# A decoder layer's sliding-window attention: the softmax reciprocals laid out in the odd slots, in a bank of the scores' ring

## The chip, the cores and the metric

The kernel runs on one core of a Trainium2 chip. The metric is the time of one execution on the device in microseconds (us); lower is better. The core's engines are TensorE (PE, with its weight loads PEld), VectorE (DVE), ScalarE (ACT), GpSimd (POOL) and SyncE (SP, which issues transfers). Each engine runs its instructions in the order of its own queue and waits there for semaphores of the others. TensorE writes its results into PSUM, of which this kernel uses eight banks of 128 x 512 float32; VectorE and ScalarE read them from there.

## The reference

One layer with two branches on x (1024 x 1024, float32). What matters here is the attention branch:

```python
proj = rmsnorm(x, norm_pre) @ w_in          # -> pool_u, pool_gate, q, k, v, attn_gate
# 8 heads of 64, 2 key/value heads, blocks of 128 queries, window 128, ALiBi bias, a sink per head
scores = einsum('bnqhgd,bnkhd->bnhgqk', q, kb) * 64 ** -0.5       # own and previous block of keys
scores = where(valid, scores + bias, -1e30)
probs = softmax(concatenate([scores, sink], -1), -1)[..., :-1]
attn_out = einsum('bnhgqk,bnkhd->bnqhgd', probs, vb) * silu(attn_gate)
pool_out = pool_mixer(pool_u, pool_w, pool_scale) * silu(pool_gate)
x = x + rmsnorm(concatenate([pool_out, attn_out], -1) @ w_out, norm_post)
```

## The kernel before

Matrix products run on pairs of float16 tensors (a high and a low part), three products for one of float32. The order of all engines' queues is the order of the program text (a manual schedule); the framework adds the semaphores.

After an opening part (norms, transposes, v, k and the first q), a loop runs over the slots s = 5 to 33. Each slot computes one projection tile (proj, L283: 24 products of 128 x 512 into one of two "acc" banks), in the order q, pool_gate, u, attn_gate, and threads a piece of the attention between. With n = (s - 5) // 2, the even slot and the odd slot behind it form pair n. In block terms, a pair does the following.

- Even slot: pv_land(n-2) (VectorE, L465) multiplies the values' product of block n-2 by what lies in cat; mask(n-1) (GpSimd, two selects L427 and L431); score_mm(n) (TensorE, L360: 24 products into four banks); then proj, and in its middle (after 12 of 24 products) `middle()`; behind proj score_land(n) (VectorE, L371 to L382, reads the four banks) and exps(n) (ScalarE, L389).
- Odd slot: turn(n) (ScalarE, L399), proj with `middle()`, pv_mm(n-1) (TensorE, L455), turn_low(n) (VectorE L404 and L411, a transposing transfer L408, and GpSimd's copy r at L413, which spreads the reciprocals of block n).

`middle()` first runs scales(): a transpose that spreads a weight block's bound (L82), then on VectorE a reduction and five tiny operations (L87, L73, L76, L77, L213), and on ScalarE the scaled copy of the weights (high_w, L219). It runs only in slots whose turn it is. Then, before the change in even slots, `divide(n - 1)`: TensorE transposes r (four transposes, L442) into a bank rb, and ScalarE copies rb, times a factor, into cat (L443). pv_land later multiplies that. Last, pool_mm (L508) runs where the pooling branch has something ready.

PSUM is dealt out like this: two "acc" banks; a ring of four under the tag "b" (`bank()`: score tiles, the pooling branch's products, half of the output); one bank "pv" for the values' product pvo and, before the change, for rb; one for spread. A ring hands its banks out in turn, and a tile waits until the last reader of its predecessor in that bank is done.

Of the kernel before, what the change touches and what calls it, by code (L numbers as in the profile page):

```python
# [9 lines left out]
F32 = mybir.dt.float32  # L10
# [9 lines left out]
P = 128  # L20
# [3 lines left out]
NB = S // P  # L24
# [11 lines left out]
def trunk(ctx: ExitStack, tc, x, w_in, pool_w, pool_scale, attn_sinks, w_out, norm_pre, norm_post, out):  # L36
# [16 lines left out]
    ps_pv = ctx.enter_context(tc.tile_pool(name="ps_pv", bufs=1, space=PSUM))  # L53
# [11 lines left out]
    def block_of(n):  # L65
        return slice(n * P, (n + 1) * P)

    def bank(name, n=512):
        return ps_b.tile([P, 512], F32, tag="b", name=name)[:, :n]
# [10 lines left out]
    def spread(m):  # L80
        t = ps_sp.tile([P, 512], F32, tag="sp", name="spread")[:, :P]
        nc.tensor.transpose(t, m.broadcast_to([P, P]), ident)  # L82
        return t

    def widest(t):
        a = col("amall")
        nc.vector.tensor_reduce(a, t, axis=AX.X, op=ALU.max)  # L87
        return a
# [132 lines left out]
    def low_w(ch):  # L221
        w, s = whl[ch], halves.pop(ch)
        nc.vector.scalar_tensor_tensor(  # L223
            w[:, 1], raws.pop(ch), s, w[:, 0], op0=ALU.mult, op1=ALU.subtract
        )
# [126 lines left out]
    def score_mm(n):  # L352
        k0 = 0 if n else 1
        for pr in range(2):
            banks = [bank("sc").rearrange("p (c b s) -> p c b s", c=2, b=2) for _ in range(2)]
            for ci in range(2):
                for i, (a, b) in enumerate(PASSES):
                    for kv in range(2):
                        rows = slice(kv * HD, (kv + 1) * HD)
                        nc.tensor.matmul(  # L360
                            banks[kv][:, ci, k0:, :],
                            qT[rows, a, 2 * pr + ci, block_of(n)],
                            kT[rows, b, (n - 1 + k0) * P : (n + 1) * P],
                            start=i == 0, stop=i == 2,
                        )
            att_sc[n, pr] = banks
# [29 lines left out]
    def turn(n):  # L396
        st, sums = att_s.pop(n)
        ph = att.tile([P, 2, 8, P], F16, tag="ph", name="ph")
        nc.scalar.activation(ph[:, 0], st[:, :, :P], AF.Copy, scale=4096.0)  # L399
        att_f[n] = (st, sums, ph)  # L400
# [19 lines left out]
    def mask(n):  # L420
        full = att_f.pop(n)
        if n == 0:
            att_p[n] = [(0, full)]
            return
        own = att.tile([P, 2, 8, P], F16, tag="own", name="own")
        f, o = (t.rearrange("p a j t -> p (a j) t") for t in (full, own))
        nc.gpsimd.affine_select(  # L427
            o, f, pattern=[[0, 16], [1, P]], compare_op=ALU.is_ge, fill=0.0,
            base=0, channel_multiplier=-1,
        )  # L430
        nc.gpsimd.affine_select(  # L431
            f, f, pattern=[[0, 16], [-1, P]], compare_op=ALU.is_ge, fill=0.0,
            base=-1, channel_multiplier=1,
        )
        att_p[n] = [(n, own), (n - 1, full)]


    def divide(n):
        r = att_r.pop(n)
        rb = ps_pv.tile([P, 512], F32, tag="pv", name="rb")  # L440
        for c in range(4):
            nc.tensor.transpose(rb[:, block_of(c)], r[:, block_of(c)], ident)  # L442
        nc.scalar.activation(  # L443
            cat[:, 4:8, block_of(n)], rb.rearrange("p (c t) -> p c t", t=P), AF.Copy, scale=vo
        )
# [17 lines left out]
    def pv_land(n):  # L463
        dst, pv = cat[:, 4:8, block_of(n)], att_o.pop(n)
        nc.vector.tensor_tensor(dst, pv.rearrange("p (c t) -> p c t", t=P), dst, op=ALU.mult)  # L465
# [18 lines left out]
    def pool_windows(c, half):  # L484
        ug = pool_in.pop((c, half))
        w = WINDOWS[c]
        cur, d = ug, 1
        while d < w:
            nxt = strip("win")
            lo = 2 * d - 1  # L490
            nc.vector.tensor_tensor(
                nxt[:, lo:], cur[:, lo:], cur[:, lo - d : PAD + 512 - d], op=ALU.add
            )
            cur = nxt
            d *= 2
        res = strip("res")[:, PAD:]
        nc.vector.scalar_tensor_tensor(
            res, cur[:, PAD:], 1.0 / w, ug[:, PAD:], op0=ALU.mult, op1=ALU.subtract
        )
        if half == 0:  # L500
            first = slice(PAD, PAD + w - 1)
            nc.vector.tensor_tensor(cur[:, first], cur[:, first], invc[:, : w - 1], op=ALU.mult)
            nc.vector.tensor_tensor(res[:, : w - 1], cur[:, first], ug[:, first], op=ALU.subtract)
        pool_out[c, half] = res
# [140 lines left out]
    with tc.manual_schedule(engines={ENG.PE, ENG.Activation, ENG.DVE, ENG.Pool, ENG.SP}):  # L645
# [125 lines left out]
        def load_next():  # L771
            ch = next(loads, None)
            if ch:
                load_w(ch)
# [9 lines left out]
        for s in range(5, last):  # L784
            ch, half = slots[s]
            n, odd = (s - 5) // 2, (s - 5) % 2
            if not odd:
                if 2 <= n <= NB + 1:
                    pv_land(n - 2)
                if 1 <= n <= NB:  # L790
                    mask(n - 1)
                if n < NB:
                    score_mm(n)
            elif n < NB:
                turn(n)
            if 20 <= s < 24:
                gate = cat[:, s - 20, :]
                nc.scalar.activation(gate, gate, AF.Silu)
            gates = list(pool_out)

            def sums():
                for key in list(pool_in):
                    pool_windows(*key)


            def lows():
                for c2 in list(halves):
                    low_w(c2)
                    load_next()


            def scales():
                for key in list(bounds):
                    if key[0] in ("wo", "c"):
                        spreads[key] = spread(bounds.pop(key))
                        if key[0] == "c":
                            scale_cat(key[1])
                        else:
                            pow2_of(widest(spreads.pop(key)), wop, wos, 14)
                            state["wo"] = True  # L820
                    elif first_slot[key] == s + 3:
                        spread_w((key,))
                        scale_w((key,))
                        high_w(key)

            def middle():
                if s < LATE:
                    scales()
                if not odd and 1 <= n <= NB:
                    divide(n - 1)  # L830
                for key in gates:
                    pool_mm(*key)

            ready = list(halves)
            if s < LATE:
                sums()
                lows()
                acc = proj(ch, half, middle)
            else:
                acc = proj(ch, half, middle, scales)  # L840
                sums()
                for c2 in ready:
                    low_w(c2)
                    load_next()
                if s >= 26 and wo_lo < wo_hi:
                    low_wo(wo_lo)
                    wo_lo += 1
            if odd and 1 <= n <= NB:
                pv_mm(n - 1)
            if odd and n < NB:  # L850
                turn_low(n)

            for c2 in order:
                if first_slot[c2] == s + 5:
                    bound_w(c2)

            if 9 <= s < 9 + KT:
                wo_raw["b", s - 9] = load_wo(s - 9)
            if 11 <= s < 11 + KT:
                bound_wo(s - 11)  # L860
            if s == 11 + KT:
                m = bounds["wo", 0] = col("wom")
                nc.vector.tensor_reduce(m, wom, axis=AX.X, op=ALU.max)
            if s >= 30:
                bound_cat(s - 30)
            if not odd and n < NB:
                score_land(n)
            for key in gates:
                pool_gate(*key)
            land_slot(ch, half, acc)  # L870
            if s >= 23 and wo_hi < KT:
                split_wo(wo_hi)
                wo_hi += 1
            if not odd and n < NB:
                exps(n)
            if s == 5 + 2 * NB + 1:
                open_late()
            if 21 <= s < 21 + KT:
                wo_raw["o", s - 21] = load_wo(s - 21)
            if s >= last - 2:  # L880
                load_res(s - last + 2)
# [47 lines left out]
```

## Time and profile before

| | |
|---|---|
| time, median of the runs | 342.42 us (lowest 341.96) |
| profiled execution | 341.63 us, its span 339.9 us |
| TensorE busy | 322.6 us, 95% of the span |
| VectorE, ScalarE, GpSimd busy | 198.3, 169.6, 66.1 us |
| chain that ended last | TensorE 60%, issue 14%, VectorE 10%, GpSimd 8%, ScalarE 5% |

The loop of slots with attention in them lies between about 61 and 190 us; the rest of the projections run to 250 us, and the output product to 335 us. Matmuls are pipelined, so the sum of their single times is more than the stretch they take; the start of one to the start of the next is the measure. In a timeline row the number in brackets is the engine's idle time just ahead of it, with the instruction that ended it.

### The profile page before, as it was taken

What the parts mean: (1) busy time and instruction counts of PE and PEld (TensorE: products, weight loads), DVE (VectorE), ACT (ScalarE), POOL (GpSimd) and SP (SyncE); (2) the same over time, 40 slices, a digit from 0 to 9 for tenths busy, and PEclk for the clock granted to TensorE, in tenths of its full rate; (3) what the DMA queues carried; (4) which work ended last, traced back from release to release, by engine and by line L of the source; (5) the groups of instructions that cost most, each with busy time, mean ns of one, the idle gap of its engine ahead of it and who ended that gap; (6) DMA issues with size and microseconds to landing.
All of it is one profiled execution on the core that took longest, in us unless ns stands there. A gap on an engine that the chain in (4) does not pass through costs nothing.

```text
span 339.9 us, 5053 instructions
## 1 busy us (share of the span) xinstructions
PE 322.6 (95%) x1913; PEld 166.8 (49%) x1913; DVE 198.3 (58%) x423; ACT 169.6 (50%) x368; POOL 66.1 (19%) x73
## 2 busy tenths in 40 slices
PE   4789999999999999999979999999999999999993
PEld 2688556545445445454434444444444444444442
DVE  4977871537697444796979678833753633310122
ACT  5867831275657675888394573326543442211011
POOL 1101303000142343132405000000000233312330
PEclk9999999999999999999999999999999999999999
DMA  8976240002437376385631690320000341133111
GB/s 279 275 212 189 70 125 0 2 15 49 123 123 183 129 188 152 85 165 117 104 78 46 215 263 20 114 73 0 2 0 0 103 147 67 61 120 123 62 64 62
DMA packets 52090, 35.73 MB, mean 105 GB/s; under 512 B 35041, under 2 KB 45793, under 8 KB 52066
## 3 DMA queue, kind: packets, MB, share of 16 engines
q1 hardware_dynamic: 52064, 35.40, 38.2%
q8 instruction: 15, 0.25, 0.3%
q14 instruction: 9, 0.07, 0.1%
q10 hardware_dynamic: 2, 0.00, 0.0%
HBM read 27.01 MB, written 4.19 MB: 92 GB/s over the span
## 4 chain that ended last, share of the span: by engine, by line
PE 60%; issue 14%; DVE 10%; POOL 8%; ACT 5%; DMA 2%; POOLq 0%; DVEq 0%; ACTq 0%
PE acc L292 41%; POOL o L641 5%; PE pv L272 3%; PE y L272 3%; ACT st L389 3%; PE tp L250 2%; PE sc L360 2%; PE pvo L455 2%; PE mixed L508 2%; PE acc L272 2%; DVE o L638 2%; DMA full<-ph 1%; DVE st L377 1%; PE gain L176 1%; POOL yf L633 1%
## 5 line engine op out<-in xcount | busy, mean ns | idle before, releaser
L292 PE MATMUL acc<-hT,whl 128*128 128x512 f16 x792 | 177.1, 379 | 0.0
L292 PEld LDWEIGHTS <-whl 128*128 128x128 f16 x792 | 76.6, 98 | 91.9 <-issue 6.9
L272 PE MATMUL y<-wo,chl 128*128 128x512 f16 (+2 forms) x408 | 83.6, 366 | 0.0
L272 PEld LDWEIGHTS <-chl 128*128 128x128 f16 x408 | 39.0, 98 | 43.5
L611 ACT ACTIVATE junk<-y 128x512 bf16<-128x512 f32 (+2 forms) x17 | 9.7, 572 | 54.9 <-PE y L272 54.9
L389 ACT ACTIVATE st<-st,negm 128x129 f32<-128x129 f32 x64 | 24.8, 390 | 12.6 <-DVE negm L382 9.5
L613 DVE SCALAR_TENSOR_TENSOR eps_of<-yss,eps_of 128x1 f32<-128x1 f32 x17 | 3.2, 186 | 45.9 <-ACT junk L611 45.9
L219 ACT ACTIVATE whl<-wraw,ws 128x1024 f16<-128x1024 f32 x18 | 20.4, 1145 | 15.9 <-DVE ws L77 12.3
L633 POOL TENSOR_TENSOR yf<-eps_of,mhalf 128x1 f32<-128x1 f32 x7 | 3.8, 549 | 115.1 <-DVE eps_of L613 115.1
L223 DVE SCALAR_TENSOR_TENSOR whl<-wraw,ws,whl 128x1024 f16<-128x1024 f32 x18 | 23.7, 1325 | 0.0
L404 DVE SCALAR_TENSOR_TENSOR ph<-st,ph 128x1024 f16<-128x1024 f32 x8 | 9.8, 1226 | 21.8 <-ACT ph L399 21.8
L641 POOL TENSOR_TENSOR o<-o,xr 128x512 f32<-128x512 f32 x14 | 17.5, 1268 | 9.1 <-DVE o L638 9.1
L91 ACT ACTIVATE whl<-wraw 128x1024 bf16<-128x1024 f32 x18 | 18.8, 1049 | 0.6 <-DMA wraw<-in_w_in_dram 0.6
L427 POOL TENSOR_SCALAR_AFFINE_SELECT own<-full 128x2048 f16<-128x2048 f16 x7 | 14.5, 2072 | 22.9 <-DMA full<-ph 22.9
L413 POOL COPY r<-sums 128x512 f32<-128x512 f32 x8 | 4.9, 610 | 67.8 <-DVE sums L411 45.8
L250 PE MATMUL tp<-ident,h 128*128 128x128 f32 x64 | 11.7, 350 | 5.9 <-DVE h L241 3.4
L95 DVE SCALAR_TENSOR_TENSOR chl<-cat,cs,chl 128x1024 f16<-128x1024 f32 x8 | 10.3, 1285 | 10.2 <-ACT chl L94 10.2
L377 DVE SCALAR_TENSOR_TENSOR st<-sc,qu,bias 128x256 f32<-128x256 f32 x32 | 15.2, 484 | 1.0
L531 ACT ACTIVATE gt<-acc,wu 128x512 f32<-128x512 f32 x8 | 5.5, 687 | 18.9 <-PE acc L292 15.4
L431 POOL TENSOR_SCALAR_AFFINE_SELECT full<-full 128x2048 f16<-128x2048 f16 x7 | 14.4, 2052 | 0.5
L94 ACT ACTIVATE chl<-cat,cs 128x1024 f16<-128x1024 f32 x8 | 9.2, 1147 | 10.0 <-DVE cs L77 10.0
L250 PEld LDWEIGHTS tp<-ident,h 128*128 128x128 f32 x64 | 9.9, 182 | 7.3 <-DVE h L241 3.8
(109 smaller groups left out, 377.0 us busy)
## 6 DMA issues: line engine op xcount, KB each, us to landing
wraw<-in_w_in_dram SPq DMA_DIRECT2D x10, 512.0 KB, 5.1
x<-in_x_dram SPq DMA_DIRECT2D x8, 512.0 KB, 5.2
wraw<-in_w_in_dram SPq DMA_DIRECT2D x16, 256.0 KB, 4.7
woraw<-in_w_out_dram SPq DMA_DIRECT2D x8, 512.0 KB, 5.6
woraw<-in_w_out_dram SPq DMA_DIRECT2D x16, 256.0 KB, 7.0
xr<-in_x_dram SPq DMA_DIRECT2D x8, 512.0 KB, 3.5
out_dram<-o SPq DMA_DIRECT2D x16, 256.0 KB, 2.0
post<-in_norm_post_dram SPq DMA_DIRECT2D x1, 512.0 KB, 4.6
```

The lines of the kernel that those rows point to most:

```text
L91: nc.scalar.activation(junk, src, AF.Abs, accum_out=m)
L95: eng.scalar_tensor_tensor(lo, src, s, hi, op0=ALU.mult, op1=ALU.subtract)
L219: nc.scalar.activation(whl[ch][:, 0], raws[ch], AF.Copy, scale=halves[ch])
L223: nc.vector.scalar_tensor_tensor(w[:, 1], raws.pop(ch), s, w[:, 0], op0=ALU.mult, op1=ALU.subtract)
L250: nc.tensor.transpose(flips[tt][b][:, block_of(i)], h[:, block_of(4 * b + i)], ident)
L272: nc.tensor.matmul(acc, a, b, start=i == 0, stop=i == len(pairs) - 1)
L292: nc.tensor.matmul(acc, w[:, a, k, :], hT[:, b, k, half_of(half)], start=k == 0 and i == 0, stop=k == KT - 1 and i == 2,)
L377: nc.vector.scalar_tensor_tensor(st[:, hs, :P], sc[:, :, 0 if n else 1, :], qu[:, 2 * pr : 2 * pr + 1], (bias if n else bias0)[:, hs, :], ...
L389: nc.scalar.activation(st[:, h, :], st[:, h, :], AF.Exp, bias=negm[:, h : h + 1], accum_out=sums[:, h : h + 1],)
L427: nc.gpsimd.affine_select(o, f, pattern=[[0, 16], [1, P]], compare_op=ALU.is_ge, fill=0.0, base=0, channel_multiplier=-1,)
L431: nc.gpsimd.affine_select(f, f, pattern=[[0, 16], [-1, P]], compare_op=ALU.is_ge, fill=0.0, base=-1, channel_multiplier=1,)
L641: nc.gpsimd.tensor_tensor(o[:, hs], o[:, hs], xr[:, hs], op=ALU.add)
```

## The change

Two lines. The bank of rb comes from the ring "b" instead of "pv", and divide(n - 1) is called in the middle of the odd slot of pair n instead of its even slot.

```diff
     def divide(n):
         r = att_r.pop(n)
-        rb = ps_pv.tile([P, 512], F32, tag="pv", name="rb")
+        rb = bank("rb")
         for c in range(4):
             nc.tensor.transpose(rb[:, block_of(c)], r[:, block_of(c)], ident)
...
             def middle():
                 if s < LATE:
                     scales()
-                if not odd and 1 <= n <= NB:
+                if odd and 1 <= n <= NB:
                     divide(n - 1)
                 for key in gates:
                     pool_mm(*key)
```

ScalarE, pairs 1 and 2, from the odd slot of pair 1 on (ph is turn's output, whl a scaled weight block, qT and cat take accumulators, st the scores); one piece of the difference:

```order
 L399 ACTIVATE ph<-st 128x1024
 L219 ACTIVATE whl<-wraw,ws 128x1024
+L443 ACTIVATE cat<-rb,vo 128x4x128
 L91 ACTIVATE whl,as<-wraw 128x1024
 L94 ACTIVATE qT<-acc 128x512
 L219 ACTIVATE whl<-wraw,ws 128x1024
-L443 ACTIVATE cat<-rb,vo 128x4x128
 L94 ACTIVATE qT<-acc 128x512
 L389 ACTIVATE st,sums<-st,negm 128x129 x8
 L399 ACTIVATE ph<-st 128x1024
 L219 ACTIVATE whl<-wraw,ws 128x1024
+L443 ACTIVATE cat<-rb,vo 128x4x128
```

The copy L443 has moved from a place ahead of the exponentials of the even slot to one behind turn (and behind high_w, where a weight block is scaled) of an odd slot.

TensorE, even slot of pair 2, around the middle of the scores: 1166, 1167, 1180 and 1181 are the four score tiles in their order, qT the weights. Before:

```order
L360 MATMUL sc_1167<-kT_105,qT_104 128x256
L360 LDWEIGHTS qT_104
L360 MATMUL sc_1180<-kT_105,qT_104 128x256 [waits DVE_49]
L360 LDWEIGHTS qT_104
L360 MATMUL sc_1181<-kT_105,qT_104 128x256 [waits DVE_49]
```

and now:

```order
L360 MATMUL sc_1167<-kT_105,qT_104 128x256
L360 LDWEIGHTS qT_104 [waits DVE_49]
L360 MATMUL sc_1180<-kT_105,qT_104 128x256 [waits PE_49]
L360 LDWEIGHTS qT_104
L360 MATMUL sc_1181<-kT_105,qT_104 128x256 [waits Activation_49]
```

The first product into the fourth tile, the 14th of the 24, waited for VectorE and now waits for ScalarE; it is the same in pairs 2 to 7.

TensorE, the transposes of block 0, in the middle of a slot's products (acc) and behind a spread. Before, in the even slot of pair 1:

```order
L292 LDWEIGHTS whl_326
L292 MATMUL acc_1033<-hT_102,whl_326 128x512
L82 MATMUL spread_1046<-ident_95,as_946 128x128 [waits Activation_49]
L442 MATMUL rb_1058<-ident_95,r_998 128x128 [waits Pool_49]
L442 MATMUL rb_1058<-ident_95,r_998 128x128 x3
L292 LDWEIGHTS whl_326
```

and now, in its odd slot:

```order
L292 LDWEIGHTS whl_546
L292 MATMUL acc_1101<-hT_102,whl_546 128x512
L82 MATMUL spread_1114<-ident_95,as_1001 128x128 [waits DVE_49,Activation_49]
L442 MATMUL rb_1126<-ident_95,r_998 128x128 [waits DVE_49,PE_49,Pool_49]
L442 MATMUL rb_1126<-ident_95,r_998 128x128 x3
L292 LDWEIGHTS whl_546
```

The transposes moved by one slot; they wait for the ring's bank as well as for r. The queues of VectorE, GpSimd and SyncE keep their order; on VectorE L465 now waits for ScalarE's L443 too.

## Rows read from the trace of the kernel before

**Rows 1.** The page, busy time of the engines (share of span, instructions).
```profile
PE 322.6 (95%) x1913; PEld 166.8 (49%) x1913; DVE 198.3 (58%) x423; ACT 169.6 (50%) x368; POOL 66.1 (19%) x73
```

**Rows 2.** Busy time by stretch: engines' us and counts, granted clock, DMA share, GB/s.
```profile
6.00:8.00 2.00, 0.25 (x3) 0.17 (x1) 1.34 (x5) 1.37 (x3) 0.25 (x1) 1.00 1.10 380
...
174.00:177.00 3.00, 1.19 (x6) 0.34 (x5) 1.97 (x6) 2.99 (x5) 0.61 (x1) 1.00 0.51 118
...
200.00:250.00 50.00, 50.00 (x230) 23.06 (x229) 32.67 (x59) 22.98 (x30) 0.00 (x0) 1.00 0.20 56
```

**Rows 3.** Timeline of TensorE: start, duration, line, op, tiles, count, idle before.
```profile
87.04 1.48 PE L360 MATMUL sc<-kT,qT 64*128 64x256 f16 x24
...
92.08 0.63 PE L442 MATMUL rb<-ident,r 128*128 128x128 f32 x4 [0.75 <-DVE cat L465]
...
101.94 1.48 PE L360 MATMUL sc<-kT,qT 64*128 64x256 f16 x24
...
106.31 0.66 PE L442 MATMUL rb<-ident,r 128*128 128x128 f32 x4 [0.19 <-POOL r L413]
...
116.08 1.48 PE L360 MATMUL sc<-kT,qT 64*128 64x256 f16 x24
...
143.77 1.48 PE L360 MATMUL sc<-kT,qT 64*128 64x256 f16 x24
...
157.72 1.48 PE L360 MATMUL sc<-kT,qT 64*128 64x256 f16 x24
...
177.03 0.63 PE L442 MATMUL rb<-ident,r 128*128 128x128 f32 x4 [1.84 <-DVE cat L465]
```

**Rows 4.** Timeline of ScalarE, odd slots of pairs 1, 2, 3, 5, 6.
```profile
87.00 1.06 ACT L399 ACTIVATE ph<-st 128x1024 f16<-128x1024 f32 x1
87.96 1.13 ACT L219 ACTIVATE whl<-wraw,ws 128x1024 f16<-128x1024 f32 x1
89.00 1.04 ACT L91 ACTIVATE whl<-wraw 128x1024 bf16<-128x1024 f32 x1
...
103.08 1.06 ACT L399 ACTIVATE ph<-st 128x1024 f16<-128x1024 f32 x1
...
115.41 1.06 ACT L399 ACTIVATE ph<-st 128x1024 f16<-128x1024 f32 x1
...
143.47 1.06 ACT L399 ACTIVATE ph<-st 128x1024 f16<-128x1024 f32 x1
...
157.09 1.06 ACT L399 ACTIVATE ph<-st 128x1024 f16<-128x1024 f32 x1
```

**Rows 5.** Groups of instructions by line: busy us, mean ns of one, idle before.
```profile
L443 ACT ACTIVATE cat<-rb,vo 128x512 f32<-128x512 f32 x8 | 5.4, 678 | 5.8 <-PE rb L442 5.8
```

**Rows 6.** Timeline of VectorE.
```profile
93.82 1.24 DVE L213 TENSOR_TENSOR wu<-wp,gsc 128x1 f32<-128x1 f32 x1
...
134.14 0.29 DVE L87 TENSOR_REDUCE amall<-spread 128x1 f32<-128x128 f32 x1 [3.52 <-PE spread L82]
...
134.92 0.52 DVE L213 TENSOR_TENSOR wu<-wp,gsc 128x1 f32<-128x1 f32 x1
...
148.88 0.14 DVE L213 TENSOR_TENSOR wu<-wp,gsc 128x1 f32<-128x1 f32 x1
...
159.46 0.67 DVE L465 TENSOR_TENSOR cat<-pvo,cat 128x512 f32<-128x512 f32 x1
...
176.21 0.67 DVE L465 TENSOR_TENSOR cat<-pvo,cat 128x512 f32<-128x512 f32 x1
```

**Rows 7.** Timeline of GpSimd.
```profile
93.05 2.00 POOL L427 TENSOR_SCALAR_AFFINE_SELECT own<-full 128x2048 f16<-128x2048 f16 x1 [2.88 <-DMA full<-ph]
...
133.43 2.00 POOL L427 TENSOR_SCALAR_AFFINE_SELECT own<-full 128x2048 f16<-128x2048 f16 x1 [3.08 <-DMA full<-ph]
...
150.16 2.00 POOL L427 TENSOR_SCALAR_AFFINE_SELECT own<-full 128x2048 f16<-128x2048 f16 x1 [3.19 <-DMA full<-ph]
```

**Rows 8.** Waits from 172 to 190 us: total us, times, longest.
```profile
PEld mixed L508 <- DVE res L503: 0.3, 1, 0.3
```

## What the change will do to the time, predicted before it ran

> **What bounds the kernel now.** I read the page's busy shares first, then TensorE's waits, then its timeline from 70 to 190 us, and last the other engines just ahead of each wait. TensorE (PE) is busy 322.6 of 339.9 us [rows 1], and from 200 to 250 us it has no gap at all [rows 2]: every microsecond it gains or loses in the slots before that is a microsecond of the end, as long as nothing else comes level with it. In the slots that hold the attention it waits three times, each time for the bank of the reciprocals: at 92.08 us (0.75 us) and at 177.03 us (1.84 us) the transposes of L442 wait for VectorE's product L465, which must leave the single "pv" bank first, and at 106.31 us they wait 0.19 us for GpSimd's copy r [rows 3]. Together that is 2.78 us, the most that the change can give back: 0.8% of the time.
>
> **What the change adds.** Call pair n the even slot that runs score_mm(n) and the odd slot behind it. Before, the reciprocals of block n-1 lay in a bank of their own kind; now they take a fifth tile per pair out of a ring of four. score_mm of pair n takes all four, so its last tile is the bank that rb took one odd slot earlier, and it may be written only when ScalarE (ACT) has copied rb out (L443). The order shows that: the 14th of the 24 score products, which waited for VectorE, now waits for ACT. And that copy has moved too: it no longer stands early in the even slot but behind the exponentials, turn(n) and, where a weight block is being scaled, high_w. In-order ACT cannot pull it forward. So the question for each pair is whether L443 ends before PE reaches the 14th product.
>
> **Two clocks per pair.** In score_mm the 24 products take 1.48 us, 59 ns each, so the 14th comes 0.77 us after the start given in [rows 3]. On ACT, turn (L399) of the odd slot starts as in [rows 4]; the next operation follows 0.96 us later (87.00 to 87.96), the one behind high_w 1.04 us after that (87.96 to 89.00), and L443 itself lasts 0.68 us [rows 5]. I add 0.1 us for the signal, between nothing and the 0.15 us that PE took from the end of a VectorE product (176.21 + 0.67) to its start at 177.03 [rows 6]. So the bank is free 2.78 us after turn starts where high_w stands between them, 1.74 us after it where not.
>
> Pair 2: turn at 87.00, bank free at 89.78; PE there at 87.04 + 0.77 = 87.81. **Stall 1.97 us.** Nothing on ACT or VectorE has moved yet, so this term is the safest.
>
> Pair 3: PE comes 1.97 us late out of pair 2 and saves the 0.75 us wait at 92.08, so it is 1.22 us late. ACT's work behind the moved L443 starts some 0.6 us later than before, and VectorE with it, but VectorE loses nothing: the tiny product L213 at 93.82 lasted 1.24 us and ended at 95.06, just as GpSimd's select that began at 93.05 ended (95.05); the same product took 0.14 us at 148.88, ahead of the next select at 150.16 [rows 6, 7]. I take it that L213 waits for the select's end in either kernel, so the exponentials and turn keep their time (103.08). Bank free at 105.86; PE at 101.94 + 0.77 + 1.22 = 103.93. **Stall 1.93 us**, PE now 3.15 us late.
>
> Pairs 4 and 5: the wait of 0.19 us goes, PE is 2.96 us late. No weight block is scaled in these odd slots. Turn of pair 3 stood at 115.41, and slips about 0.5 us since ACT lands the accumulator of its even slot later; the bank is free near 117.7, PE arrives at 116.08 + 0.77 + 2.96 = 119.81. **No stall**, with 2 us in hand, and the same in pair 5: ACT's work there follows PE's accumulators, so a late PE makes both late.
>
> Pair 6: VectorE starts the scores' landing of pair 5 only behind the spread that PE makes in the middle of that even slot; it had waited 3.52 us for it at 134.14 [rows 6]. So its whole chain, the exponentials and turn (143.47) shift by PE's 2.96 us. In before's times the bank is free at 146.25 and PE there at 144.54, 1.71 us apart; both shift alike, less the 0.38 us by which L213 at 134.92 (0.52 against 0.14 us) was held by the select of 133.43. **Stall 1.33 us**, PE 4.29 us late.
>
> Pair 7: again the spread gates VectorE. In before's times turn at 157.09 frees the bank at 159.87 and PE is there at 158.49: 1.38 us. But L213 of that slot stood at 148.88, ahead of the select at 150.16; PE and VectorE are now 4.3 us late and the select only 2.6 (it hangs on pair 5's turn, 2.96 less 0.38). L213 then issues at 153.2 into a select that runs from 152.7 to 154.7, and loses 1.45 us. **Stall 2.8 us**, PE 7.1 us late.
>
> The Trainium skill (SBUF — State Buffer, "Who interferes with whom") says that a VectorE instruction with two SBUF inputs and a GpSimd one that reads SBUF lock each other out for a whole instruction. By that rule L213 waits as I have it, and the two rows agree; by a reading without it pair 7 costs 1.4 us less.
>
> After pair 7 no scores come. The 1.84 us wait at 177.03 goes, which would leave 5.3 us. But VectorE is later than that: its product L465 of block 5 stood at 159.46 [rows 6] and now waits for the late copy's end, 165.5, so the chain behind it is about 6.1 us late, and PE was already level with it before, waiting 0.3 us for VectorE's res in the odd slot of that stretch [rows 8]. So PE takes over that lateness: **about +6.2 us** from 190 us on, and nothing behind gives it back.
>
> The other parts cost nothing of their own. The four transposes (0.6 us) and L443 are as many as before. r is ready long before its new place in the odd slot (GpSimd copies it in the first third of the even slot). The bank that rb takes was last read by VectorE's second landing operation, 1.5 us or more ahead of the middle of the odd slot. pv_mm no longer waits for ACT, and did not lose by it. Were that cover gone, rb would wait for VectorE in the odd slot by the same fraction of a microsecond as it does now in the even one (0.19 to 0.75 us).
>
> **The sum.** 1.97 + 1.93 + 1.33 + 2.8 = 8.0 us of new stalls, less 2.8 us of old ones, plus 0.9 us of the late VectorE chain: 6.2 us. On the profiled execution's own 341.63 us that is 347.8 us; the timed runs of before lie 0.3 to 0.8 us above it (341.96 lowest, 342.42 median), so I forecast 348.3 us, 1.8% slower. A measurement of this kernel tells about 2% (6.8 us) from no change, so this counts as the same, but only just.
>
> **Rivals.** First, the change does what it looks like: a bank of another ring is simply free, and the 2.78 us are gained: 338.9 us by the profile. The Trainium skill (Perfetto Trace Analysis, "Matmuls" under Optimizing Tensor Performance) speaks for it: independent groups should rotate through different banks so that one is emptied under the next. Against it: the ring has four banks for five tiles, and in pair 2 no change of order upstream can move ACT's copy ahead of 89.0 us. The Trainium skill (Perfetto Trace Analysis, "Optimization Strategy") speaks against it: bubbles that repeat on the busiest engine can mean too little PSUM for the next tile. Chance 0.04.
>
> Second, no lock-out in pair 7: the stall there is 1.4 us and the VectorE chain 4.7 us late: 346.3 us. For it speaks that the select and L213 must overlap within half a microsecond. Chance 0.21.
>
> Third, the other side of 2%: a lock-out in pair 5 as well. There L213 issues at 137.9 us and GpSimd's first select ends at 133.43 + 2.4 + 2.00 = 137.8, its second starting 0.07 us later and lasting 2 us. If L213 comes after that start, pair 6's stall grows by 1.9 us and all behind it: 349.7 us, 2.4% slower. It is decided by a tenth of a microsecond at 137.8. Chance 0.28.
>
> Fourth, PE's clock: a stalled engine might be granted the lower of its levels, 1.2 instead of 2.4 GHz. The next half slot of 12 products (2.6 us) would take 2.6 us more, four times over 10 us: 358 us. Against it: between 6 and 8 us PE was busy 0.25 of 2 us, and at 174 to 177 us 1.19 of 3, at a granted clock of 1.00 both times [rows 2]. Chance 0.03.
>
> **The numbers.** The forecast, with no lock-out in pair 5 and one in pair 7, has 0.40; what is left over, 0.04, are stalls in pairs 4 or 5 that I don't see. The second rival, the forecast and the third cover 346.3 to 349.7 us by the profile; with 0.1 us of signal up or down per stall, the offset of the timed runs at the top, and at the bottom PE not taking over VectorE's 0.9 us, that is 345.0 to 351.0 us, which holds about 0.85 of the chance. Without the rivals the forecast's own range is 347.3 to 349.3. Faster by over 2%: 0.01, since only 2.8 us can be gained. Slower by over 2%: the third rival, the fourth, the unseen stalls and a tenth of the forecast's own spread, 0.28 + 0.03 + 0.04 + 0.04 = 0.39. Within 2%: 0.60.
>
> **What would show it.** In the profile after: no wait of rb for L465; a wait of the scores (L360) for ACT's L443 in pairs 2, 3, 6 and 7, of 1.3 to 2.8 us each, none in pairs 4 and 5; L213 at about 153 us lasting over 1 us; granted clock 1.00 throughout. The forecast is wrong if the scores show no such wait, if pairs 4 and 5 stall as well, or if PE's lateness at 190 us is given back before the end.

## The result, and the profile after

The changed kernel takes 353.77 us (median, runs from 351.62 to 354.66) against 342.42 us of the kernel before measured beside it (median of three; a fourth run of it, at 1195.05 us, is not counted): a ratio of 1.0325, 95% interval 1.0301 to 1.0348. It is 5.5 us slower than the 348.3 us forecast and lies outside the range of 345.0 to 351.0. Its profiled execution took 353.92 us, span 352.2 us, 12.3 us more than the span of before.

The waits of TensorE over the whole span (engine, what waited, for whom: total us, times, longest), in the trace after:

```profile
PE sc L360 <- ACT cat L443: 8.3, 4, 2.8
...
PE mixed L508 <- DVE res L503: 1.2, 1, 1.2
```

The waits of rb for VectorE and GpSimd [rows 3] are gone. In their place the scores wait for ScalarE's copy four times, and the wait of [rows 8] has grown. The timeline of TensorE in the trace after shows where (start, duration, line, operation, tiles, count, idle before):

```profile
87.27 0.93 PE L360 MATMUL sc<-kT,qT 64*128 64x256 f16 x13
89.96 0.81 PE L360 MATMUL sc<-kT,qT 64*128 64x256 f16 x11 [1.75 <-ACT cat L443]
90.70 4.45 PE L292 MATMUL acc<-hT,whl 128*128 128x512 f16 x12
...
108.62 1.43 PE L360 MATMUL sc<-kT,qT 64*128 64x256 f16 x11 [2.77 <-ACT cat L443]
109.99 8.84 PE L292 MATMUL acc<-hT,whl 128*128 128x512 f16 x36
...
123.21 1.48 PE L360 MATMUL sc<-kT,qT 64*128 64x256 f16 x24
...
152.93 0.81 PE L360 MATMUL sc<-kT,qT 64*128 64x256 f16 x11 [1.10 <-ACT cat L443]
153.68 2.76 PE L292 MATMUL acc<-hT,whl 128*128 128x512 f16 x12
...
169.78 1.38 PE L360 MATMUL sc<-kT,qT 64*128 64x256 f16 x11 [2.63 <-ACT cat L443]
171.10 7.06 PE L292 MATMUL acc<-hT,whl 128*128 128x512 f16 x27
...
195.84 1.10 PE L508 MATMUL mixed<-res,pw 128*128 128x512 f32 x2 [1.16 <-DVE res L503]
```

Two things are to be read here. The scores of [rows 3] are cut after 13 products in pairs 2, 3, 6 and 7, and run through in pair 4 (and 5), as the ring says. And the work behind three of the four waits is itself slow: 12 products of 128 x 512 take 2.76 us behind the wait of 1.10 us, but 4.45 us behind that of 1.75 us; the 11 score products take 0.81 us in pairs 2 and 6, but 1.43 and 1.38 us in pairs 3 and 7. The granted clock tells why (stretch, its length, PE, PEld, VectorE, ScalarE, GpSimd busy with counts, then the clock, DMA share, GB/s):

```profile
88.00:90.00 2.00, 0.25 (x5) 0.04 (x3) 1.34 (x2) 2.00 (x4) 0.21 (x1) 1.00 0.54 162
90.00:92.00 2.00, 2.00 (x16) 1.08 (x16) 0.54 (x1) 1.43 (x3) 0.41 (x1) 0.84 0.74 169
92.00:94.00 2.00, 2.00 (x6) 0.70 (x5) 1.94 (x3) 0.00 (x0) 0.71 (x1) 0.50 0.42 93
...
110.00:112.00 2.00, 2.00 (x7) 0.75 (x7) 1.93 (x6) 0.19 (x2) 0.00 (x0) 0.54 1.51 80
...
154.00:156.00 2.00, 2.00 (x11) 0.88 (x10) 0.80 (x1) 1.53 (x3) 0.00 (x0) 1.00 1.31 194
...
170.00:172.00 2.00, 2.00 (x14) 0.96 (x11) 1.08 (x2) 1.51 (x4) 0.23 (x1) 0.50 0.76 173
```

Behind the waits of pairs 2, 3 and 7 TensorE is granted 1.2 GHz (0.50) for a stretch, in pair 2 once the score products are through and in pairs 3 and 7 from these on, and it counts as busy all the while; behind that of pair 6 it keeps 2.4 GHz (1.00).

### The profile page after: what moved, and what is told of

The parts are those of the page before. It is cut to its first block, busy times and chain, and to the rows that moved or that the text cites. A ratio compares the mean times of both kernels' runs of the same rounds, so it can differ in the third digit from the quotient of the medians.

```text
span 352.2 us, 5063 instructions
## 1 busy us (share of the span) xinstructions
PE 327.3 (93%) x1913; PEld 167.8 (48%) x1913; DVE 201.4 (57%) x423; ACT 169.1 (48%) x368; POOL 67.7 (19%) x73
## 4 chain that ended last, share of the span: by engine, by line
PE 57%; issue 14%; DVE 14%; ACT 7%; POOL 6%; DMA 0%; POOLq 0%; DVEq 0%; ACTq 0%
PE acc L292 40%; POOL o L641 5%; ACT st L389 3%; PE pv L272 3%; PE y L272 3%; PE sc L360 3%; DVE st L377 2%; PE acc L272 2%; PE tp L250 2%; PE mixed L508 2%; PE pvo L455 2%; DVE sc L376 2%; DVE o L638 1%; DVE negm L382 1%; ACT whl L219 1%
## 5 line engine op out<-in xcount | busy, mean ns | idle before, releaser
L292 PE MATMUL acc<-hT,whl 128*128 128x512 f16 x792 | 180.6, 385 | 0.0
L292 PEld LDWEIGHTS <-whl 128*128 128x128 f16 x792 | 77.5, 99 | 95.0 <-issue 11.8
L223 DVE SCALAR_TENSOR_TENSOR whl<-wraw,ws,whl 128x1024 f16<-128x1024 f32 x18 | 22.8, 1277 | 0.0
L360 PE MATMUL sc<-kT,qT 64*128 64x256 f16 (+1 forms) x192 | 13.9, 279 | 8.9 <-ACT cat L443 8.3
L427 POOL TENSOR_SCALAR_AFFINE_SELECT own<-full 128x2048 f16<-128x2048 f16 x7 | 16.1, 2293 | 24.3 <-DMA full<-ph 24.3
L250 PE MATMUL tp<-ident,h 128*128 128x128 f32 x64 | 9.9, 306 | 6.9 <-DVE hT L261 3.5
L360 PEld LDWEIGHTS <-qT 64*128 64x128 f16 x192 | 9.1, 98 | 14.2 <-issue 11.8
L87 DVE TENSOR_REDUCE amall<-spread 128x1 f32<-128x128 f32 x25 | 7.1, 285 | 13.4 <-PE spread L82 13.3
```

Source lines behind the costliest of these rows:

```text
L223: nc.vector.scalar_tensor_tensor(w[:, 1], raws.pop(ch), s, w[:, 0], op0=ALU.mult, op1=ALU.subtract)
L250: nc.tensor.transpose(flips[tt][b][:, block_of(i)], h[:, block_of(4 * b + i)], ident)
L292: nc.tensor.matmul(acc, w[:, a, k, :], hT[:, b, k, half_of(half)], start=k == 0 and i == 0, stop=k == KT - 1 and i == 2,)
L360: nc.tensor.matmul(banks[kv][:, ci, k0:, :], qT[rows, a, 2 * pr + ci, block_of(n)], kT[rows, b, (n - 1 + k0) * P : (n + 1) * P], start=i = ...
L427: nc.gpsimd.affine_select(o, f, pattern=[[0, 16], [1, P]], compare_op=ALU.is_ge, fill=0.0, base=0, channel_multiplier=-1,)
```

## Experiments

### The slot alone, and the bank alone

Each half of the change was run by itself, the rest as before:

```diff
-                if not odd and 1 <= n <= NB:
+                if odd and 1 <= n <= NB:
```

> Only the place of the transposes and of their copy moves to the odd slot; rb stays in the one bank of the values' product. Theory (the late copy L443 is the cause, whichever bank it holds): now the values' product waits for L443, since it takes the same bank at the end of the odd slot. That stands 1.5 to 2.2 us ahead of the 14th score product, so the waits are longer than in the changed kernel (2.6 to 3.6 us in pairs 1, 2, 5 and 6), with TensorE at half clock behind them: 356 to 366 us. Rival (the bank out of the scores' ring is the cause): without it the stalls are gone, 339 to 343 us.

```diff
-        rb = ps_pv.tile([P, 512], F32, tag="pv", name="rb")
+        rb = bank("rb")
```

> Only the bank changes to the ring of the scores; the transposes stay in the even slot. Theory (five tiles in four banks): rb takes the first score bank of its own pair, which VectorE empties only behind the middle of the even slot, so rb waits 2 to 4 us for L377 in pairs 1, 2, 3, 5, 6 and 7, while the scores no longer wait for L443: 349 to 358 us. Rival (the slot is the cause, not the bank): 339 to 343 us, like the kernel before or a little faster.

Measured: the slot alone 369.58 us (1.0800, interval 1.0768 to 1.0832), the bank alone 355.73 us (1.0398, interval 1.0369 to 1.0427). The waits of TensorE in each, that of the slot first:

```profile
PE pvo L455 <- ACT cat L443: 22.3, 6, 5.1
```

```profile
PE rb L442 <- DVE st L377: 12.6, 5, 2.9
```

Neither half gains anything. With the slot alone the values' product of the same slot needs the single bank that ScalarE's late copy still reads, in six odd slots; the time lies above the expected 356 to 366 us because the odd slots of pairs 3 and 7 pay too (2.94 and 5.12 us), where in the changed kernel the ring gives the copy until the 14th score product of the next pair, or for good. With the bank alone the fifth tile falls on a bank that VectorE is still landing, as expected, though in five pairs and not in six (pair 3 has no wait). So a place behind the exponentials on ScalarE is dear in either bank, and the ring only makes it cheaper: 369.58 down to 353.77.

### The copy put first on ScalarE

The changed kernel, with the reciprocals' copy issued ahead of the exponentials and turn in pairs 1 to 6 (these move from behind the even slot into the middle of the odd one, and the weights' scaling goes behind them; the lines that are taken out elsewhere are not shown):

```diff
             def middle():
-                if s < LATE:
-                    scales()
                 if odd and 1 <= n <= NB:
                     divide(n - 1)
+                if odd and 1 <= n <= 6:
+                    exps(n)
+                    turn(n)
+                if s < LATE:
+                    scales()
```

> The changed kernel, with the exponentials and turn of pairs 1 to 6 issued on ScalarE behind the copy L443 instead of ahead of it. Theory (the stall is the copy's place behind exponentials, turn and high_w on ScalarE): L443 ends about 1 us after the transposes, some 2.5 us ahead of the next scores; no wait of the scores, clock 1.00 in all slots, 339 to 342 us, so 0 to 2.8 us below the kernel before. Rival (a fifth tile in a ring of four costs stalls wherever the copy stands): 348 us or more.

Measured 342.05 us (1.0002, interval 0.9978 to 1.0027; runs from 340.99 to 344.64), at the upper edge of the 339 to 342 us expected. ScalarE's rows, first of the changed kernel, then of this one, in the same pair:

```profile
87.23 1.06 ACT L399 ACTIVATE ph<-st 128x1024 f16<-128x1024 f32 x1
88.20 1.13 ACT L219 ACTIVATE whl<-wraw,ws 128x1024 f16<-128x1024 f32 x1
89.24 0.67 ACT L443 ACTIVATE cat<-rb,vo 128x512 f32<-128x512 f32 x1
```

```profile
84.93 0.69 ACT L443 ACTIVATE cat<-rb,vo 128x512 f32<-128x512 f32 x1 [2.05 <-PE rb L442]
85.51 0.39 ACT L389 ACTIVATE st<-st,negm 128x129 f32<-128x129 f32 x1
```

The copy ends at 85.62 instead of 89.91 us, before the scores of pair 2 begin, and no score product waits for it any more. This settles the first half of the explanation: the 8.25 us of stalls come from the copy's place in ScalarE's queue. Yet the kernel is no faster than before, though the old waits of 2.78 us are gone too. The timeline of TensorE, further on, shows what took them in the profiled execution:

```profile
184.23 1.63 PE L508 MATMUL mixed<-res,pw 128*128 128x512 f32 x2 [2.32 <-DVE res L503]
185.65 3.96 PE L292 MATMUL acc<-hT,whl 128*128 128x512 f16 x12
```

The pooling branch's product in the odd slot of pair 8 waits 2.32 us for VectorE, and the 12 products behind it take 3.96 us instead of 2.76: the gain returns as one wait and its stretch at half clock. The profiled execution, at 344.03 us, was one of the two slowest of ten, however. Four of the others took 340.99 to 341.43 us, about 1 us less than the kernel before. The first of these shows a mean granted clock of 0.999 (0.984 in the profiled one), which leaves some 0.7 us at half clock in all. That, and the 3 us between the two times, speak against the stretch being there each time; only the profiled execution left a trace.

### The waits filled with work

The changed kernel, with 7, 8, 4 and 8 additional products of 128 x 512 (their result is used nowhere) ahead of the 14th score product of pairs 2, 3, 6 and 7:

```diff
+                        if (pr, ci, i, kv) == (1, 0, 0, 1) and n in FILL:
+                            w = whl[slots[5 + 2 * n][0]]
+                            fill = ps_sp.tile([P, 512], F32, tag="sp", name="fill")
+                            for _ in range(FILL[n]):
+                                nc.tensor.matmul(
+                                    fill, w[:, 0, 0, :], hT[:, 0, 0, half_of(0)], ...
```

> The changed kernel with 7, 8, 4 and 8 more products of 128 x 512 on TensorE ahead of the 14th score product of pairs 2, 3, 6 and 7, into the spread's bank, read by nobody: work that isn't part of the computation, 0.216 us each, so 1.5, 1.7, 0.9 and 1.7 us, less than the waits there. Theory (of the 11 us about 5 are TensorE's lower clock behind the waits): the waits shrink by as much, the granted clock stays at 1.00 behind them, and the time falls to 347 to 350 us, although work was added. Rival (the clock costs nothing, the waits do all): 353 to 355 us, unchanged, or longer by what doesn't fit.

Measured 349.84 us (1.0232, interval 1.0206 to 1.0258), within the 347 to 350 us expected. TensorE's bank is free hardly earlier than in the changed kernel, but TensorE is busy for most of the time until then; its timeline in pairs 2, 3 and 7 (line 370 is the former 360, 365 the additional products):

```profile
88.86 1.69 PE L365 MATMUL fill<-hT,whl 128*128 128x512 f16 x7
90.68 0.81 PE L370 MATMUL sc<-kT,qT 64*128 64x256 f16 x11
91.42 2.76 PE L292 MATMUL acc<-hT,whl 128*128 128x512 f16 x12
...
104.82 1.90 PE L365 MATMUL fill<-hT,whl 128*128 128x512 f16 x8
107.27 0.81 PE L370 MATMUL sc<-kT,qT 64*128 64x256 f16 x11 [0.55 <-ACT cat L453]
108.02 7.94 PE L292 MATMUL acc<-hT,whl 128*128 128x512 f16 x36
...
166.60 0.81 PE L370 MATMUL sc<-kT,qT 64*128 64x256 f16 x11 [0.49 <-ACT cat L453]
167.34 6.00 PE L292 MATMUL acc<-hT,whl 128*128 128x512 f16 x27
```

The 11 score products take 0.81 us again, 12 products 2.76 instead of 4.45 us, 36 take 7.94 instead of 8.84, 27 take 6.00 instead of 7.06. Useless work made the kernel 3.9 us faster by the medians: what it bought is the clock. The profiled executions reach the loop at 63.1 to 64.4 us, whatever the kernel, so two of them are better compared from the same score product on (at 63.34 and at 64.06 us): from there to the end of the span they take 288.9 and 283.2 us. The clock's price in the changed kernel is thus 4 to 6 us. The rest of the slowdown, 7.6 us by the medians and 6.4 us by the same comparison with the kernel before (276.8 us from 63.10 on), is the waits themselves, filled or not.

### VectorE's tiny product out of the way of GpSimd

The changed kernel, with L213 as a tensor by a scalar:

```diff
-        nc.vector.tensor_tensor(u, p, gsc, op=ALU.mult)
+        nc.vector.tensor_scalar(u, p, gsc[:, 0:1], None, op0=ALU.mult)
```

> The changed kernel, with the tiny product L213 written as a tensor by a scalar read through a pointer instead of a tensor by a tensor. Theory (L213 with two tensors from SBUF cannot start during a GpSimd select): L213 now takes 0.2 us or less everywhere, VectorE's chain in pairs 2 and 6 ends about 1.6 us earlier, so the stalls of the scores in pairs 3 and 7 fall from 2.8 and 2.6 to 1.0 to 1.6 us, those in pairs 2 and 6 stay; 3 us less of stalls and perhaps 1 to 3 us less of half clock behind them: 347.5 to 351.5 us. Rival (L213 is held by something else, such as the chain ahead of it): it stays long, 352.5 to 355 us.

Measured 353.25 us (1.0348, interval 1.0300 to 1.0397), the same as the changed kernel within the spread: the expectation of 347.5 to 351.5 us was wrong, and the stalls of pairs 3 and 7 fell only to 2.31 and 2.45 us, not to between 1.0 and 1.6. VectorE and GpSimd's selects around 94 and 155 us in this kernel, then the same two places in the changed one:

```profile
93.22 2.46 POOL L427 TENSOR_SCALAR_AFFINE_SELECT own<-full 128x2048 f16<-128x2048 f16 x1 [2.94 <-DMA full<-ph]
94.52 0.20 DVE L213 TENSOR_SCALAR wu<-wp,gsc 128x1 f32<-128x1 f32 x1
94.63 1.09 DVE L371 COPY st<-sinks 128x8 f32<-128x8 f32 x1
...
154.82 2.00 POOL L427 TENSOR_SCALAR_AFFINE_SELECT own<-full 128x2048 f16<-128x2048 f16 x1 [3.17 <-DMA full<-ph]
155.28 0.20 DVE L213 TENSOR_SCALAR wu<-wp,gsc 128x1 f32<-128x1 f32 x1
155.39 1.47 DVE L371 COPY st<-sinks 128x8 f32<-128x8 f32 x1
```

```profile
95.87 2.00 POOL L431 TENSOR_SCALAR_AFFINE_SELECT full<-full 128x2048 f16<-128x2048 f16 x1
96.08 1.81 DVE L213 TENSOR_TENSOR wu<-wp,gsc 128x1 f32<-128x1 f32 x1
97.81 0.16 DVE L371 COPY st<-sinks 128x8 f32<-128x8 f32 x1
...
157.03 2.00 POOL L427 TENSOR_SCALAR_AFFINE_SELECT own<-full 128x2048 f16<-128x2048 f16 x1 [3.31 <-DMA full<-ph]
157.37 1.67 DVE L213 TENSOR_TENSOR wu<-wp,gsc 128x1 f32<-128x1 f32 x1
```

L213 is free as expected, and the next instruction, a copy of eight numbers a row, lasts until the select ends (95.72 against 95.68 us, 156.86 against 156.82). The Trainium skill (SBUF — State Buffer, "Who interferes with whom") states both cases: an instruction with two inputs from SBUF contends with a GpSimd one that reads SBUF, and a copy can enter a mode that takes the shared ports and contend too. The trace agrees in both (1.81 and 1.67 us against 0.14 for L213, 1.09 and 1.47 against 0.16 for L371). The lock-out predicted for pair 7 is thus real, but its price can't be taken away at L213 alone. What the stall of pair 7 would be without any lock-out wasn't tried.

### A version that beats both, and its controls

First the copy-first kernel with the reciprocals in the old bank:

> As the run e3_copy_first (exponentials and turn of pairs 1 to 6 stand behind the copy L443 on ScalarE, the transposes in the odd slot), but the reciprocals' tile lies in the single bank pv as before the change. Theory (what counts is where ScalarE's copy stands in its queue, and not which bank the tile has): the copy ends early in the odd slot in either bank, so pvo (L455) does not wait for it, and the time is that of e3_copy_first, 341 to 344 us, with the wait of mixed (L508) on VectorE near 184 us. Rival (the ring's bank is what makes the odd slot possible): pvo waits for L443 as in e1_slot_alone, six times 3 to 5 us, 355 us or more.

Measured 345.96 us (1.0113, interval 1.0083 to 1.0143), outside of what was expected. TensorE waits once:

```profile
175.11 1.49 PE L455 MATMUL pvo<-own,vst 128*64 128x512 f16 x6 [5.40 <-ACT cat L443]
```

That is the odd slot of pair 7, the one in which the exponentials, turn and the gates' activation still stood ahead of the copy. In pairs 1 to 6, where the copy was first, the old bank costs no wait at all. So the theory holds for the pairs that were changed, and the expected time was wrong because pair 7 was overlooked: there the ring's bank does help.

Then the copy-first kernel in the ring's bank, with the product that waited 2.32 us moved behind its slot:

```diff
-                for key in gates:
-                    pool_mm(*key)
+                if s != 22:
+                    for key in gates:
+                        pool_mm(*key)
...
                 acc = proj(ch, half, middle, scales)
+                if s == 22:
+                    for key in gates:
+                        pool_mm(*key)
```

> As e3_copy_first, and in the one odd slot of pair 8 the pooling branch's product (L508) is issued behind the slot's 24 products instead of behind 12 of them. Theory (the 1.84 us that the change saves come back in that slot as a wait of mixed for VectorE, 2.3 us and a stretch of half clock behind it): that wait goes, VectorE is not late for the next slot, and the time is 337.5 to 340 us, the first kernel below the one before the change. Rival (VectorE's chain is the bound there): the wait moves to the next slot's mixed or pvo, 341 to 344 us.

> As e7_copy_first_mixed_late, with L213 as in e6_no_lockout. Theory (with the copy early no wait of TensorE hangs on VectorE's chain in pairs 1 to 7): no difference from e7_copy_first_mixed_late beyond 0.7 us. Rival (VectorE's lateness still counts somewhere): 1 to 3 us less than it.

> The kernel before, and only the one product L508 of the odd slot of pair 8 issued behind its slot, as in e7_copy_first_mixed_late; the reciprocals stay in the even slots and in the old bank. Theory (the 2.8 us of e7 come from the old waits for the values' product, and the late product only keeps them from coming back): the waits of 0.75 and 1.84 us stay, only the 0.3 us of the old mixed wait can go: 341.6 to 342.6 us. Rival (the place of that product is a gain of its own): 339 to 341 us.

Measured: 339.38 us with the copy first and the product late (0.9915, interval 0.9900 to 0.9931); 339.73 us with L213 changed too (0.9923, interval 0.9902 to 0.9944); and the late product alone, on the kernel before, 342.64 us (0.9997, interval 0.9983 to 1.0011). The gain of 0.85% is less than 2%, but its interval excludes no change. In the first of them TensorE's timeline has no wait behind 64 us; at the place in question:

```profile
180.87 0.60 PE L442 MATMUL rb<-ident,r 128*128 128x128 f32 x4
183.89 1.02 PE L508 MATMUL mixed<-res,pw 128*128 128x512 f32 x2
184.84 0.84 PE L455 MATMUL pvo<-own,vst 128*64 128x512 f16 x6
```

The first two came out as the theory said; the third lies 0.04 us above its range and equals the kernel before measured beside it (342.63 us), its waits of 0.75 and 1.84 us still there. The old waits were worth their 2.8 us after all (342.19 to 339.38), but only with two more moves: the copy ahead of the exponentials, and the next consumer of VectorE's late chain half a slot later. L213 makes no difference where no wait hangs on VectorE.

### Which waits cost the clock

> The changed kernel once more, for a second profile. Theory (whether TensorE's clock falls behind a given wait isn't settled by the wait's length): the waits of the scores are the same four within 0.5 us, but the stretches of half clock behind them are not the same ones as in the first profile, and their sum accounts for the difference of the spans. Rival (the length decides): half clock again behind the waits of 1.75, 2.77 and 2.63 us and not behind that of 1.10.

> The kernel before once more, for a second profile. Theory: the wait of 1.84 us at 177 us is there again; whether half clock stands behind it this time is open. Rival (waits at that place never cost clock, because of the work ahead of them): full clock behind it again.

The second profile of the changed kernel (354.23 us) shows waits of 1.75, 2.76, 1.10 and 2.44 us and half clock behind the same three; the second one of the kernel before (342.16 us) shows 1.84 us at 177.53 and full clock behind it again. So in these second profiles the guess that the stretches change from one execution to the next did not come true, and what was seen is what the rival (the length decides) had said. Yet the timed runs, of which there is no trace, speak for it. The copy-first kernel seems to have done without its stretch in one of them, as told above. Of the changed kernel's timed runs one shows 0.989 in 351.62 us, against 0.979 in 353.92 for the profiled one: about 7 us less at half clock (0.010 of 350 us, twice), more than the 3.4 us that the profile shows ahead of the loop. So whether a stretch repeats stays open.

And length alone does not decide either. The waits of over a microsecond in the odd and even slots, in all profiles:

| kernel | wait, us | behind it |
|---|---|---|
| after (both profiles) | 1.75, 2.76 to 2.77, 2.44 to 2.63 | half clock |
| after (both profiles) | 1.10; 1.15 to 1.16 | full |
| waits filled | 1.05 | full |
| L213 as a tensor by a scalar | 1.10, 1.15 | full |
| before (both profiles, and with the late product) | 1.84 | full |
| L213 as a tensor by a scalar | 1.80 | full |
| L213 as a tensor by a scalar | 2.31, 2.45 | half clock |
| bank alone | 2.04, 2.60 | half clock |
| bank alone | 2.42, 2.87, 2.71 | full |
| copy first | 2.32 | half clock |
| slot alone | 2.94, one of 3.38 | full |
| slot alone | the other 3.38, 3.67, 3.78, 5.12 | half clock |
| copy first, old bank | 5.40 | half clock |

No wait up to 1.16 us was followed by half clock. From 1.75 us on some were and some were not: a wait of 1.75 us cost what one of 2.87 us did not, and the same wait of pair 2 (1.75 and 1.80 us) went one way in the changed kernel and the other in that with the other L213. What decides among them was not found; the traces leave it open.

## Why the prediction was wrong

**What held.** The waits stand where the ring and ScalarE's order put them: pairs 2, 3, 6 and 7, none in pairs 4 and 5; the copy-first run shows that their cause is the copy's place. Their sizes, predicted and measured: 1.97 and 1.75, 1.93 and 2.77, 1.33 and 1.10, 2.8 and 2.63 us, in sum 8.0 and 8.25. That the sums agree so closely is in part luck: pair 3 was 0.84 us too small and the other three some 0.2 us too large each. L213 fell into the select in pair 6's slot (1.67 us) and just missed it in pair 5's (0.14 us at 142.05), so the forecast's case and not the third rival's, though by 0.08 us only: the second select began at 142.13. The old waits of 2.78 us went. The late VectorE chain took 0.9 us of TensorE in the forecast, 1.16 us in the trace. By these terms alone the sum is 8.25 - 2.78 + 1.16 = 6.6 us, close to the forecast's 6.2.

**The step that failed** is the fourth rival, TensorE's clock: it was named and given a chance of 0.03, so the sum has no term for it, and it happened. The three stretches cost, against the same products at full clock, 4.45 - 2.76 = 1.7 us in pair 2, (1.43 - 0.81) + (8.84 - 7.94) = 1.5 us in pair 3, and (1.38 - 0.81) + (7.06 - 6.00) = 1.6 us in pair 7: 4.8 us. With them the sum is 11.5 us of the 12.3; 0.2 us arise before 64 us, and some 0.6 us remain unexplained. The rival's own price, 2.6 us four times over, was too high: the clock came back before the 12 products of the half slot had all run at the lower level, and not every wait lost it.

Two pieces of evidence were set against that rival [rows 2], and the first of them was none. From 6 to 8 us the clock column reads 1.00 at a busy share of an eighth, but TensorE's own rows show that it did not run at full speed there. Its transposes of the opening part, first in the trace before and then in the one after:

```profile
9.67 1.97 PE L250 MATMUL tp<-ident,h 128*128 128x128 f32 x8 [3.42 <-DVE h L241]
...
14.88 1.94 PE L250 MATMUL tp<-ident,h 128*128 128x128 f32 x8 [1.16 <-DVE hT L261]
```

```profile
9.66 1.97 PE L250 MATMUL tp<-ident,h 128*128 128x128 f32 x8 [3.42 <-DVE h L241]
...
14.87 1.22 PE L250 MATMUL tp<-ident,h 128*128 128x128 f32 x8 [1.51 <-DVE hT L261]
```

The same eight transposes take 1.94 to 1.97 us at first and 1.22 us later, at a clock column of 1.00 in both stretches. In these traces the column says nothing ahead of the first change that it records, and in the trace before it stays at 1.00 up to 338 us (0.77 from there to the end). The four transposes of 0.63 us at 177.03 [rows 3] gave the measure already in the trace of before: eight in 1.97 us are slow. The second piece was sound, a wait of 1.84 us with full clock behind it, though it is the duration of those transposes and not the column that shows it; but it was one case, and the table above has waits of 1.75, 2.04 and 2.32 us that ended otherwise. One case of a wait that costs nothing could not carry a chance of 0.03 for four new waits, three of them longer by its own forecast.

**One term was mis-sized:** pair 3, by 0.84 us, and it has two halves. In the kernel with the filled waits, where the clock kept its level in pair 2 and L213 is as in the changed one, the 14th score product of pair 3 stands 2.4 us behind the end of the 13th, against 2.77 us in the changed kernel and 1.93 in the forecast. So 0.4 us follow from the clock: the slow products of pair 2 delayed the spread, and L213 met GpSimd's second select (1.81 us, ending at 97.89) instead of the first one's end. The other 0.4 to 0.5 us is there with the clock at its level too, and it is the forecast's step that VectorE comes later but loses nothing, because the select's end stays where it was. The select's end moved. VectorE's L223, first before the change and then after it with the select behind it:

```profile
91.85 1.28 DVE L223 SCALAR_TENSOR_TENSOR whl<-wraw,ws,whl 128x1024 f16<-128x1024 f32 x1
```

```profile
92.67 1.28 DVE L223 SCALAR_TENSOR_TENSOR whl<-wraw,ws,whl 128x1024 f16<-128x1024 f32 x1
93.29 2.52 POOL L427 TENSOR_SCALAR_AFFINE_SELECT own<-full 128x2048 f16<-128x2048 f16 x1 [2.88 <-DMA full<-ph]
```

Before, L223 ended as the select began (93.13 and 93.05 us), and the select took 2.00 us [rows 7]. Now L223, 0.8 us later, runs 0.66 us into the select, which takes 2.52 us. In the filled kernel an overlap of 0.65 us goes with 2.51 us, and there L213 waits for that later end (95.35 to 96.54 us, the select to 96.52); with L213 as a tensor by a scalar it is 0.61 and 2.46 us. That L223 holds the select fits all three; no run moved it to test that.

## What to carry to other kernels

When a tile joins a ring of buffers, count the tiles of one period against the ring, and read the copy that frees each one in the queue of the engine that makes it: what stands ahead of that copy is the stall, and moving the copy ahead of it is the cure. Price a new wait of TensorE of two microseconds or so not by its length alone but with a second case in which the products behind it run at 1.2 GHz, here 1.5 to 1.7 us more for each such wait, and check a clock column by the duration of equal instructions before it serves as evidence. When a wait is taken away, look for the next consumer of the engine that was nearly late: here it took the whole gain until it, too, was moved.

## What the runs showed of the hardware that was not expected

- TensorE's clock fell to half behind a wait of 1.75 us with TensorE busy on both sides of it, and filling such waits with useless products made the kernel 3.9 us faster by the medians.
- Similar waits in one execution (of the bank alone) went either way: behind 2.42, 2.71 and 2.87 us the clock stayed, behind 2.04 and 2.60 us it fell.
- An instruction of VectorE that no longer contends with GpSimd's select hands the hold to the next one that does: a copy of 128 x 8 elements took 1.09 and 1.47 us instead of 0.16.
- GpSimd's select took 2.46 to 2.52 us instead of 2.00 where a VectorE instruction with two tensors from SBUF ran 0.61 to 0.66 us into it.
